# Wd's sums moved to the projection stage, and the last pair of feature tiles multiplied by eight products

## The chip, the cores and the metric

The kernel runs on one core of a Trainium2 chip. The metric is the device time of one execution in microseconds (us). It was measured three times before the change: 2784.34 us is the median, with 2778.39 and 2784.58 beside it. One more execution was taken with the hardware profiler.

Five engines work side by side: TensorE (PE, matmuls; PEld is its weight load), VectorE (DVE), ScalarE (ACT), GpSimd (POOL) and SyncE (SP, which here only issues DMAs). Each runs its instructions in the order in which they were written, and waits at an instruction until its inputs are there.

## The reference

One layer of a trunk model on 2048 rows of width 1024, in float32:

```python
hn = rmsnorm(h, norm_mix[l])
z = hn @ w_in[l]
u_ssm, q, kv, gate_logits, lru_x, lru_g = jnp.split(z, splits, axis=-1)
...
mix = jnp.concatenate([y_ssm, y_nsa, y_lru], axis=-1)
h = h + mix @ w_out[l]
h = h + swiglu(rmsnorm(h, norm_ffn[l]), w_gate[l], w_up[l], w_down[l])
return rmsnorm(h, norm_final)
```

`y_ssm` comes from a diagonal recurrence (the S5 mixer), `y_nsa` from an attention in three branches, `y_lru` from a gated linear recurrence. `swiglu` is `(silu(h @ w_gate) * (h @ w_up)) @ w_down` with 2816 hidden features.

## The kernel before

**Three phases.** `phase_a` projects (`project`, line 492): `z` is made feature tile by feature tile, in passes over blocks of 512 rows, and the two recurrences and the compression of keys run beside it. `phase_b` is the attention and the output projection. `phase_c` (`mlp`, line 1675) is the last part: norm, gate and up, down, final norm. In the profiled execution they take about 0 to 584, 584 to 1370, and 1370 us to the end.

**Products in three parts.** Every operand of a large product is split into a rounded high part and a low part (float32r), and each product is three matmuls: high by high, high by low, low by high. A split costs ACT one copy and DVE or POOL one subtraction.

**Gate, up and down by seven products.** In `phase_c` a pair of feature tiles is handled as a 2 x 2 block product by Winograd's form of Strassen's scheme: seven products instead of eight, with sums of blocks on both sides. The 22 feature tiles of 128 give 11 pairs (`fp`). The 2048 rows are handled in two halves (`s`). For each half, `pair` (line 1852) makes gate and up for the 11 pairs (the gate/up stage), and `down` (line 1981) multiplies the result by Wd. `give` (line 1817) forms the seven combinations of the activations and stores them in DRAM as `gS`. The sums on the side of Wd are the same for both halves: `down_sums` (line 1836) loads two row blocks of Wd into two `nx` tiles of 512 KB, makes four differences of 128 x 512 (two on DVE, two on POOL, in `differences`, line 1708), and stores them as `wS`. It is called once for each of the 11 pairs during the gate/up stage of the first half, with due times 50 + 33 fp. `ahead` (line 1746) uses the same tiles `nx` and `t3` afterwards, and makes the seven row combinations that the second half multiplies.

**The down part.** `down` runs over groups of pairs, `GROUPS_D = (1, 2, 2, 2, 2, 2)`. In a group, `fetch` (line 1900) loads both operands of each of the seven products and splits them; `block` (line 1918) makes the products of one group for one of four row tiles in one PSUM bank and adds the bank to an accumulator `M[k, t]`: 28 banks a group. The accumulators start from the residual stream (`hS`, loaded in `totals`). In the last group `combine` (line 1955) puts the seven accumulators together to row tiles, takes their squares' sum, and `finish` (line 2005) scales them by the final norm and stores them. In the last group of the second half the order is row tile by row tile with all seven products in each (`7 * t + p`), elsewhere product by product (`4 * p + t`).

**What sets the order.** In `phase_a` and `phase_c` every call is recorded as a task with an engine, an assumed cost and a key (its due time). `Plan.run` simulates the engines with these costs: an engine that is free takes, among the tasks that are ready, the one with the lowest key. The order that comes out is the order in which instructions are written to each engine. Tiles of one name form a ring of `bufs` buffers in the order in which they were asked for; a task that takes a buffer waits until all uses of the buffer's last owner are over. In `phase_a` keys count feature units of 24 matmuls (one unit is about 5.4 us); the projection ends at 64.8. DMAs are issued on SP's queue, except a few on POOL's queue in `phase_b`: the loads of `KB` and of the query tiles, which are the first POOL instructions of that phase.

**Names in `phase_a` that matter.** `wsl` is the low part of a projection weight, split on POOL. `stage` is a ring of two tiles through which projected features go to DRAM (`qS`, `kS`, `vS`). The ring `b4` (two tiles of 128 x 1056) and the ring `sA` (two tiles of 128 x 512) serve the S5 mixer (`s5_prep`, `s5_main`).

## Time and profile before

| | us |
|---|---|
| median of three runs | 2784.34 |
| the three runs | 2784.34, 2784.58, 2778.39 |
| the profiled execution | 2778.5 |
| its span | 2776.7 |

| engine | busy us | share of the span |
|---|---|---|
| PE | 2577.2 | 93% |
| DVE | 2296.8 | 83% |
| POOL | 1376.6 | 50% |
| ACT | 1352.3 | 49% |

An engine is busy while it has an instruction in work. Matmuls overlap in the pipeline, so TensorE's busy time is not its rate: the number of matmuls in a stretch says more. A row of a timeline gives start, duration, engine, line, operation, output and inputs; in brackets stand the idle time before it and what ended it. Nearly all lines are 207, the helper that writes the recorded instructions, so groups are told apart by their tiles.

### The profile page before, as it was taken

To read this page: it belongs to the slowest core of one execution; us is meant where nothing else is said; L and a number is where in the kernel's file an instruction comes from. 1 tells how busy PE (TensorE), PEld (TensorE's weight loads), DVE (VectorE), ACT (ScalarE), POOL (GpSimd) and SP (SyncE) were. 2 spreads that over 40 slices of the span, in tenths; PEclk is the share of its full clock that TensorE was granted. 3 is DMA by queue.
4 is the path that set the end of the run, shared out by engine and by line. 5 is a ranking of instruction groups with operands and counts; after the bars stand their busy time and mean duration, and the time that the engine had idled before them with its cause. 6 is when DMAs were issued, how large, how long until landed. Compare 5 with 4: busy or idle time off the path is not lost. (4 is left out here: it accounts for less than half of the span.)

```text
span 2776.7 us, 43054 instructions
## 1 busy us (share of the span) xinstructions
PE 2577.2 (93%) x14889; PEld 2095.7 (75%) x14889; DVE 2296.8 (83%) x4480; ACT 1352.3 (49%) x2820; POOL 1376.6 (50%) x971
## 2 busy tenths in 40 slices
PE   6988889989999999998969989999998999999996
PEld 5756568777887788877758777887886888888785
DVE  8797776259898999999899999878889887877877
ACT  5662433147877777876633323344345333334433
POOL 2445441124544343443266766665466555556446
PEclk9999999979999999999989999999999999999998
DMA  5455556662212121121436665346654233326652
GB/s 170 121 157 161 148 137 199 204 171 61 70 41 64 36 64 41 41 52 41 143 105 227 242 228 198 113 145 239 214 180 148 107 107 113 104 90 235 218 200 82
DMA packets 231706, 376.11 MB, mean 135 GB/s; under 512 B 67040, under 2 KB 114912, under 8 KB 231488
## 3 DMA queue, kind: packets, MB, share of 16 engines
q1 hardware_dynamic: 185456, 339.27, 37.6%
q0 software_dynamic: 43872, 26.22, 4.7%
q10 hardware_dynamic: 2160, 7.87, 0.7%
q8 instruction: 118, 1.93, 0.3%
q14 instruction: 100, 0.82, 0.1%
HBM read 259.84 MB, written 113.44 MB: 134 GB/s over the span
## 5 line engine op out<-in xcount | busy, mean ns | idle before, releaser
L207 PE MATMUL B<-h,al 128*128 128x512 f32 x1232 | 486.7, 395 | 16.7 <-POOL al L207 11.2
L207 PE MATMUL B<-h,ah 128*128 128x512 f32 x1232 | 485.8, 395 | 16.7 <-ACT ah L207 7.1
L207 PE MATMUL B<-l,ah 128*128 128x512 f32 x1232 | 485.0, 394 | 4.5 <-DVE l L207 4.5
L207 PE MATMUL B<-l,h 128*128 128x512 f32 x1848 | 431.6, 394 | 11.7 <-POOL l L207 5.3
L207 PEld LDWEIGHTS B<-l,h 128*128 128x128 f32 x1848 | 348.0, 190 | 88.7 <-POOL l L207 8.2
L207 PEld LDWEIGHTS B<-h,al 128*128 128x128 f32 x1232 | 233.7, 190 | 72.4 <-POOL al L207 15.3
L207 PEld LDWEIGHTS B<-h,ah 128*128 128x128 f32 x1232 | 234.2, 190 | 67.0 <-ACT ah L207 8.2
L207 POOL TENSOR_TENSOR l<-raw,l 128x1024 fp32r<-128x1024 f32 (+1 forms) x84 | 195.8, 2342 | 170.2 <-ACT l L207 144.8
L207 PEld LDWEIGHTS B<-l,ah 128*128 128x128 f32 x1232 | 234.1, 190 | 54.7 <-DVE l L207 6.2
L393 DVE SCALAR_TENSOR_TENSOR ptl<-B,pth 128x512 f16<-128x512 f32 (+3 forms) x408 | 246.1, 624 | 22.4 <-ACT pth L384 21.1
L384 ACT ACTIVATE pth<-B 128x512 f16<-128x512 f32 (+3 forms) x408 | 214.4, 548 | 55.9 <-PE B L1509 31.6
L399 PE MATMUL B<-wo,mix 128*128 128x512 f32 x768 | 227.0, 412 | 4.7 <-DMA mix<-mixS 3.9
L207 ACT ACTIVATE ah<-S 128x512 fp32r<-128x512 f32 x176 | 110.4, 628 | 236.2 <-PE B L207 183.6
L207 POOL TENSOR_TENSOR U<-U,s 128x512 f32<-128x512 f32 x96 | 151.8, 1581 | 102.4 <-DVE U L207 57.3
L207 POOL TENSOR_TENSOR al<-S,ah 128x512 fp32r<-128x512 f32 x92 | 149.0, 1620 | 94.8 <-ACT ah L207 94.8
L384 ACT ACTIVATE Ps<-Ps,mn 128x1024 f32<-128x1024 f32 (+7 forms) x192 | 172.7, 902 | 41.3 <-DVE mn L1412 40.1
L399 PE MATMUL B<-KB,Q 128*128 128x384 f32 (+3 forms) x448 | 185.1, 413 | 6.4 <-DVE im L396 2.1
L207 PE MATMUL B<-hnl,wsh 128*128 128x512 f32 x448 | 183.3, 409 | 1.8 <-DVE hnl L207 1.8
L207 PE MATMUL B<-hnh,wsh 128*128 128x512 f32 x448 | 182.6, 408 | 0.5 <-ACT stage L207 0.3
L1509 PE MATMUL B<-ident,Ps 128*128 128x128 f32 x1088 | 181.1, 277 | 1.2 <-ACT Ps L384 0.8
L207 PE MATMUL B<-hnh,wsl 128*128 128x512 f32 x448 | 179.2, 400 | 0.0
L399 PE MATMUL B<-VV,ptl 128*128 128x64 f16 x1448 | 148.2, 195 | 27.8 <-DVE ptl L393 26.8
(371 smaller groups left out, 6282.1 us busy)
## 6 DMA issues: line engine op xcount, KB each, us to landing
raw<-in_wgu SPq DMA_DIRECT2D x88, 512.0 KB, 3.7
raw<-gS SPq DMA_DIRECT2D x70, 512.0 KB, 3.9
gS<-U SPq DMA_DIRECT2D x88, 256.0 KB, 2.1
raw<-wS SPq DMA_DIRECT2D x40, 512.0 KB, 4.0
gS<-s SPq DMA_DIRECT2D x66, 256.0 KB, 2.1
raw<-in_wd SPq DMA_DIRECT2D x66, 256.0 KB, 3.8
wraw<-in_wzf SPq DMA_DIRECT2D x28, 512.0 KB, 4.4
nx<-in_x SPq DMA_DIRECT2D x24, 512.0 KB, 4.5
```

Of the source, the lines that this page charges most:

```text
L207: f(*[real(x) for x in a], **{n: real(x) for n, x in k.items()})
L384: return self.S.activation(o, i, f, **k)
L393: return (eng or self.V).scalar_tensor_tensor(o, a, s, b, op0=op0, op1=op1, **k)
L399: return self.PE.matmul(o, l, r, start=start, stop=stop)
L1509: self.PE.transpose(pt.v[:, j - a], P.v[:, c:c + 128], self.ident)
```

## The change

The differences of Wd are made in `project`, after all other calls, for the first ten pairs: `self.at(WD_A[0] + WD_A[1] * fp, 0, self.down_sums, fp)`, with keys 60.0 to 60.9. Their loads and stores are issued on POOL's queue; the two loaded blocks stand in `b4` tiles, the fourth tile in `sA`. `wS` is kept for `phase_c`.

The eleventh pair (`TAIL = 10`) needs no sums of Wd: its four activation blocks are stored as they are (`eS`), and `ends` multiplies them by Wd's own rows, in eight products for two row tiles and two column halves at a time. This comes after the last group of seven-product pairs, whose `GROUPS_D` is now `(1, 2, 2, 2, 1, 2)`. The accumulators of the seven products are combined in that last group, ahead of the eleventh pair's products, and each of these is then added to a finished row tile. Two of the combinations move from POOL to DVE. Both halves now run all groups product by product. The row tiles are finished in groups of four, and the last four one by one; the first column half of every row tile but the last is multiplied by the final gain on DVE.

```diff
--- before.py
+++ after.py
@@ -42,12 +42,14 @@
 BANKS_C = {"P": 6, "tr": 2}
 STEP_C = 12 * 0.227
 LEAD_W, LEAD_R, LEAD_G, LEAD_D = 12.0, 40.0, 24.0, 14.0
-GROUPS_D = (1, 2, 2, 2, 2, 2)
+GROUPS_D = (1, 2, 2, 2, 1, 2)
+TAIL = 10
+WD_A = (60.0, 0.1)
 REST_C = 13.0
 GAIN_A = -6.5
 STEP_A = 0.01
 FIRST = ((0, 1), (1, 2), (2, 3), (3, 4))
-LAST = (11, 15)
+LAST = (15,)
 ACC_TAGS = {1: (("ah", 6), ("al", 6)) * 2, 6: (("ah", 6), ("al", 6)) * 2, 5: (("ah", 6), ("al", 6)) * 2, 2: (("S", 4),) * 4,
             7: (("s1", 2), ("s5", 2)) * 2, 3: (("th", 2), ("U2", 2)) * 2, 4: (("U3", 2),) * 2 + (("gain2", 1),) * 2}
 PC_TAGS = (("gain2", D, 1),) + tuple((f"{x}{n}", 2048, 1) for n in (6, 5) for x in "hl") \
@@ -362,6 +364,7 @@
         self.hS = [d(f"hS{i}", [128, D]) for i in range(16)]
         self.gS = [{k: [d(f"gS{s}_{k}_{g}", [128, n, 512]) for g, n in enumerate(GROUPS_D)] for k in range(1, 8)} for s in range(2)]
         self.wS = {k: [d(f"wS{k}_{g}", [128, n, 512]) for g, n in enumerate(GROUPS_D)] for k in (4, 5, 6, 7)}
+        self.eS = [d(f"eS{s}", [2, 128, 2, 512]) for s in range(2)]
         self.tS = [{n: d(f"t{n}{j}", [128, 512]) for n in ("B11", "B21", "B22", "T1", "T2", "T3", "T4")} for j in range(4)]
         self.rS = d("rS", [128, 8, 512])
         self.s5S = d("s5S", [8, 128, 1056])
@@ -450,7 +453,7 @@
 
     def phase_a(self):
         tc = self.tc
-        kept = ("gates", "vmax", "KC", "vcT", "ssq", "uS", "yS", "kcS", "kS", "qS", "vS", "mixS", "rS", "s5S", "s5T")
+        kept = ("gates", "vmax", "KC", "vcT", "ssq", "uS", "yS", "kcS", "kS", "qS", "vS", "mixS", "rS", "s5S", "s5T", "wS")
         with ExitStack() as ctx:
             pool = ctx.enter_context(tc.tile_pool(name="pa", bufs=1))
             psum = ctx.enter_context(tc.tile_pool(name="pa_ps", bufs=1, space=PSUM))
@@ -554,6 +557,33 @@
                     self.at(x - LEAD[2], 0, weights, u[0])
                 self.feat_unit(seq[u[0]], q, hq[v], ws[u[0]])
                 x += 1
+        for fp in range(TAIL):
+            self.at(WD_A[0] + WD_A[1] * fp, 0, self.down_sums, fp)
+
+    def differences(self, a0, b0, a1, b1, t3, names=("T2", "T4")):
+
+        self.tt(t3, b1, a1, OP.subtract)
+        if "T2" in names:
+            self.tt(a1, a1, a0, OP.subtract, eng=self.G)
+            self.tt(a0, a0, t3, OP.add)
+            if "T4" in names:
+                self.tt(b0, b0, a0, OP.subtract, eng=self.G)
+        else:
+            self.tt(b0, b0, a0, OP.subtract, eng=self.G)
+            self.tt(b0, b0, t3, OP.subtract)
+
+    def down_sums(self, fp):
+
+        gi, j = at_group(fp)
+        x = []
+        for i in range(2):
+            x.append(self.pool.tile([128, 1056], F32, name="b4", bufs=2)[:, :D])
+            self.G.dma_start(x[i], self.io["wd"][2 * fp + i])
+        t3 = self.w("sA", bufs=2)
+        a0, a1, b0, b1 = x[0][:, :512], x[0][:, 512:], x[1][:, :512], x[1][:, 512:]
+        self.differences(a0, b0, a1, b1, t3)
+        for k, v in ((7, t3), (5, a1), (6, a0), (4, b0)):
+            self.G.dma_start(self.wS[k][gi][:, j], v)
 
     def bcast(self, t, v):
         self.dma(t, bass.AP(tensor=v.tensor, offset=v.offset, ap=[[0, 128], [1, v.shape[0]]]))
@@ -1670,7 +1700,7 @@
             psum = ctx.enter_context(self.tc.tile_pool(name="pc_ps", bufs=1, space=PSUM, reuse_waits="tile"))
             for name, n, bufs in PC_TAGS:
                 pool.tile([128, n], F32, name=name, bufs=bufs)
-            self.recorded(pool, psum, BANKS_C, ("rstd", "ssq", "hS", "gS", "wS", "tS"), self.mlp, START_C)
+            self.recorded(pool, psum, BANKS_C, ("rstd", "ssq", "hS", "gS", "eS", "wS", "tS"), self.mlp, START_C)
 
     def mlp(self):
 
@@ -1705,16 +1735,7 @@
             self.stt(x, x, r, gain, OP.mult, OP.mult)
             return x
 
-        def differences(a0, b0, a1, b1, t3, names):
...
+        differences = self.differences
 
         def rows_a(j):
 
@@ -1811,14 +1832,14 @@
             self.act(th, g, AF.Tanh, scale=0.5)
             self.stt(g, th, 1.0, g, OP.add, OP.mult)
 
-        def at_group(fp):
-            return (0, 0) if fp == 0 else ((fp + 1) // 2, (fp + 1) % 2)
-
         def give(s, fp, r, c, g, u, G, U):
 
+            self.stt(g, g, 0.5, u, OP.mult, OP.mult)
+            if fp == TAIL:
+                self.dma(self.eS[s][c][:, r], g)
+                return
             gi, j = at_group(fp)
             keep = lambda k, x: self.dma(self.gS[s][k][gi][:, j], x)
-            self.stt(g, g, 0.5, u, OP.mult, OP.mult)
             G[r, c], U[r, c] = g, u
             if (r, c) != (0, 1):
                 keep({(0, 0): 1, (1, 0): 2, (1, 1): 4}[r, c], g)
@@ -1832,19 +1853,6 @@
             if (r, c) == (1, 0):
                 self.tt(u, g, U[1, 1], OP.subtract, eng=self.G)
                 keep(3, u)
-
-        def down_sums(fp):
-
-            gi, j = at_group(fp)
-            x = []
-            for i in range(2):
-                x.append(pool.tile([128, D], F32, name="nx", bufs=3))
-                self.dma(x[i], io["wd"][2 * fp + i])
-            t3 = pool.tile([128, 512], F32, name="t3", bufs=1)
-            a0, a1, b0, b1 = x[0][:, :512], x[0][:, 512:], x[1][:, :512], x[1][:, 512:]
-            differences(a0, b0, a1, b1, t3, ("T2", "T4"))
-            for k, v in ((7, t3), (5, a1), (6, a0), (4, b0)):
-                self.dma(self.wS[k][gi][:, j], v)
 
         PROD = {1: ("A11", "B11"), 2: ("A12", "B21"), 3: ("S4", "B22"), 4: ("A22", "T4"), 5: ("S1", "T1"), 6: ("S2", "T2"),
                 7: ("S3", "T3")}
@@ -1899,11 +1907,14 @@
 
         def fetch(s, k, gi, pos, x):
 
-            n, first, r = GROUPS_D[gi], sum(GROUPS_D[:gi]), []
+            n, first, r = 2 if k is None else GROUPS_D[gi], sum(GROUPS_D[:gi]), []
             for tag in "hl":
                 v = pool.tile([128, 2, D], F32R, name=f"{tag}{FREED[s][pos]}", bufs=1)[:, :, :512 * n]
                 raw = pool.tile([128, KT, 128], F32, name="raw", bufs=4).rearrange("p a b -> p (a b)")[:, :512 * n]
-                if tag == "h" or k in self.wS:
+                if k is None:
+                    src = self.eS[s][gi].rearrange("p a b -> p (a b)") if tag == "h" else io["wd"][2 * TAIL + gi]
+                    self.at(x - LEAD_G, 0, self.dma, raw, src)
+                elif tag == "h" or k in self.wS:
                     src = (self.gS[s] if tag == "h" else self.wS)[k][gi]
                     self.at(x - LEAD_G, 0, self.dma, raw, src.rearrange("p a b -> p (a b)"))
                 else:
@@ -1959,53 +1970,69 @@
             if k == 6:
                 tt(2, 1, G)
                 tt(6, 1)
-                tt(3, 6, G)
+                tt(3, 6)
             elif k == 5:
-                tt(3, 5, G)
+                tt(3, 5)
             elif k == 7:
                 tt(7, 6)
                 tt(4, 7, G)
                 tt(7, 5)
-            i = 8 * s + t
-            for i, dh, o, after in ((i, 0, 2, 2), (i, 1, 3, 3), (i + 4, 0, 4, 4), (i + 4, 1, 7, 7)):
-                if k == after:
-                    a, d = M[o, t], slice(512 * dh, 512 * dh + 512)
-                    acc[i, dh] = a
-                    junk = pool.tile([128, 512], BF, name="junk", bufs=1)
-                    self.at(x + .3, 0, lambda: self.act(junk, a, AF.Square, accum_out=ms[:, dh, col(i):col(i) + 1]))
-                    if i in LAST:
-                        if i not in last:
-                            last[i] = pool.tile([128, D], F32, name="nx", bufs=3)
-                        self.at(x + .3, 0, self.tt, last[i][:, d], a, gfin[dh], OP.mult, self.G if dh else None)
+        def ends(s, i, dh, hw, x):
+
+            c, t = i // 4, i % 4
+            i += 8 * s
+            a, d = M[{(0, 0): 2, (0, 1): 3, (1, 0): 4, (1, 1): 7}[c, dh], t], slice(512 * dh, 512 * dh + 512)
+            ps = psum.tile([128, 512], F32, name="P")
+
+            def products():
+                for r in range(2):
+                    g, w = hw[c][0][:, :, 512 * r + 128 * t:512 * r + 128 * t + 128], hw[r][1][:, :, d]
+                    self.mm(ps, g[:, 0], w[:, 0], r == 0, False)
+                    self.mm(ps, g[:, 0], w[:, 1], False, False)
+                    self.mm(ps, g[:, 1], w[:, 0], False, r == 1)
+
+            self.at(x, 0, products)
+            e = x + 1.362
+            self.at(e, 0, self.tt, a, a, ps, OP.add)
+            acc[i, dh] = a
+            junk = pool.tile([128, 512], BF, name="junk", bufs=1)
+            self.at(e + .3, 0, lambda: self.act(junk, a, AF.Square, accum_out=ms[:, dh, i:i + 1]))
+            if i in LAST:
+                if i not in last:
+                    last[i] = pool.tile([128, D], F32, name="nx", bufs=3)
+                self.at(e + .3, 0, self.tt, last[i][:, d], a, gfin[dh], OP.mult, self.G if dh else None)
 
         def down(s, x):
+
 
             seq = (1, 6, 5, 2, 7, 3, 4)
             totals(s, x)
             for gi, n in enumerate(GROUPS_D):
-                end = gi == len(GROUPS_D) - 1
                 u = .681 * n
-                at = lambda p, t: x + u * (7 * t + p if end and s else 4 * p + t)
-                hw = {k: fetch(s, k, gi, p, at(p, 0)) for p, k in enumerate(seq)}
-                for t, p in ((t, p) for t in range(4) for p in range(7)) if end and s else ((t, p) for p in range(7) for t in range(4)):
-                    k, y = seq[p], at(p, t)
+                hw = {k: fetch(s, k, gi, p, x + 4 * u * p) for p, k in enumerate(seq)}
+                for t, p in ((t, p) for p in range(7) for t in range(4)):
+                    k, y = seq[p], x + u * (4 * p + t)
                     block(s, k, gi, t, hw[k], y)
-                    if end:
+                    if gi == len(GROUPS_D) - 1:
                         combine(s, t, k, y + u)
-                        if s and k == 4:
-                            self.at(y + u + 1, 0, finish, 8 + t, 12 + t)
-                        elif not s and t == 3 and k in (3, 4):
-                            self.at(y + u + 1, 0.01, finish, *range(4 * (k == 4), 4 * (k == 4) + 4))
                 x += 28 * u
+            hw = [fetch(s, None, r, r, x) for r in range(2)]
+            for i in range(8):
+                for dh in range(2):
+                    ends(s, i, dh, hw, x)
+                    x += 1.362
+                if s and i > 3:
+                    self.at(x + 1, 0, finish, 8 * s + i)
+                elif i == 3 or i == 7:
+                    self.at(x + 1, .01, finish, *range(8 * s + i - 3, 8 * s + i + 1))
             return x
 
         M = {}
-        col = lambda i: i if i < 8 else 8 + 2 * (i % 4) + (i - 8) // 4
 
         def finish(*tiles):
 
             n = len(tiles)
-            c = col(tiles[0])
+            c = tiles[0]
             m = ms[:, 0, c:c + n]
             self.tt(m, m, ms[:, 1, c:c + n], OP.add)
             ys = self.rsqrt(pool, m, n, 1.0 / D, bufs=2, root=tiles[0] > 7)
@@ -2020,7 +2047,7 @@
                             self.ts(a, a, y)
                     else:
                         a = acc[i, dh]
-                        if i > 7 and dh == 0:
+                        if dh == 0:
                             self.stt(a, a, y, gfin[dh], OP.mult, OP.mult)
                         else:
                             self.act(a, a, scale=y)
@@ -2051,8 +2078,6 @@
                     plan.floor = 40.0
                     self.at(x + 60, 0.01, self.row_scales, 1, 2)
                     plan.floor = REST_C
-                if s == 0:
-                    self.at(50 + 33 * fp, 0, down_sums, fp)
                 x += 14 * STEP_C
             if s == 0:
                 for j in range(4):
@@ -2062,6 +2087,15 @@
                 for lead, names in ((26, ("B11", "B21")), (14, ("T2", "T1")), (6, ("T3", "B22")), (2, ("T4",))):
                     for j in range(4):
                         self.at(x - lead + 2 * j, 0, rows_of, j, names)
+
+
+def at_group(fp):
+
+    gi = 0
+    while fp >= GROUPS_D[gi]:
+        fp -= GROUPS_D[gi]
+        gi += 1
+    return gi, fp
 
 
 def bucket(dist):
```

## Rows read from the trace of the kernel before

**Rows 1.** The page's part 1: busy time, share of the span and instructions of each engine
```profile
PE 2577.2 (93%) x14889; PEld 2095.7 (75%) x14889; DVE 2296.8 (83%) x4480; ACT 1352.3 (49%) x2820; POOL 1376.6 (50%) x971
```

**Rows 2.** Busy time by stretch (PE, PEld, DVE, ACT, POOL, clock, DMA share, GB/s), gate/up stages
```profile
1455.00:1550.00 95.00, 95.00 (x418) 78.43 (x417) 89.83 (x98) 31.74 (x55) 66.63 (x43) 0.99 0.68 232
...
1550.00:1700.00 150.00, 135.64 (x569) 107.20 (x568) 138.29 (x139) 39.88 (x72) 106.47 (x66) 0.98 0.69 234
...
1700.00:1850.00 150.00, 150.00 (x663) 124.20 (x662) 128.57 (x143) 52.94 (x91) 90.52 (x59) 1.00 0.36 120
...
2130.00:2500.00 370.00, 370.00 (x1634) 306.35 (x1633) 297.85 (x336) 128.38 (x218) 209.69 (x139) 1.00 0.31 109
```

**Rows 3.** Wd's sums in the first gate/up stage: issues by tile (ns, first to last), DMAs
```profile
L207 SPq DMA_DIRECT2D wS<-t x11: 319/327/327, 1459.3 to 1610.2; - x11
...
nx<-in_wd SPq DMA_DIRECT2D x22, 512.0 KB, 4.2
...
wS<-nx SPq DMA_DIRECT2D x33, 256.0 KB, 2.5
```

**Rows 4.** Groups of 1460 to 1700 us that write nx and t: busy, mean ns, idle before
```profile
L207 DVE TENSOR_TENSOR nx<-nx,t 128x512 f32<-128x512 f32 x15 | 15.6, 1041 | 5.5 <-POOL nx L207 5.5
...
L207 DVE SCALAR_TENSOR_TENSOR nx<-nx,rstd,gain 128x1024 f32<-128x1024 f32 x8 | 14.8, 1846 | 4.6 <-DMA nx<-hS 4.6
...
L207 DVE TENSOR_TENSOR t<-nx 128x512 f32<-128x512 f32 x14 | 11.5, 823 | 0.2
...
L207 POOL TENSOR_TENSOR nx<-nx 128x512 f32<-128x512 f32 x30 | 46.4, 1546 | 37.0 <-DVE nx L207 24.9 <-DVE t L207 10.7 <-PE B L207 1.4
```

**Rows 5.** Late projection: busy time by stretch; TensorE's longest wait there; one row of ACT
```profile
366.00:440.00 74.00, 63.93 (x319) 52.98 (x317) 59.57 (x67) 29.05 (x44) 33.40 (x19) 0.93 0.64 167
...
366.00:584.00 218.00, 199.03 (x1085) 167.39 (x1083) 105.72 (x157) 58.09 (x115) 50.47 (x32) 0.96 0.63 179
...
PE B L207 <- DVE l L207: 15.0, 2, 9.3
...
553.11 0.60 ACT L207 ACTIVATE stage<-B 128x512 fp32r<-128x512 f32 x1 [10.70 <-DMA qS<-stage]
```

**Rows 6.** Last matmuls of the S5 mixer; KB's loads on POOL's queue, first use, landing
```profile
L207 PE MATMUL B<-sA,w_glu x12: 590/592/592, 359.8 to 365.2; 128*128 128x512 f32 x12
...
539.37 3.07 POOL L1089 DMA_DIRECT2D KB<-kS  x4
...
L399 PE MATMUL B<-KB,Q x24: 415/454/582, 589.5 to 619.3; 128*128 128x128 f32 x16, 128*128 128x256 f32 x8
...
KB<-kS POOLq DMA_DIRECT2D x2, 1536.0 KB, 14.3
```

**Rows 7.** One group of the second gate/up stage: DVE adding a PSUM bank
```profile
L207 DVE TENSOR_TENSOR U<-B,U 128x512 f32<-128x512 f32 x38 | 25.8, 679 | 1.2 <-POOL U L207 1.2
```

**Rows 8.** From the first half to the second, in order of time
```profile
2111.23 3.43 DVE L207 TENSOR_TENSOR S<-raw 128x512 f32<-128x512 f32 x2
...
2112.02 0.74 PE L207 MATMUL B<-h,ah 128*128 128x512 f32 x1 [2.45 <-ACT ah L207]
...
2112.55 0.63 PE L207 MATMUL B<-l,ah 128*128 128x512 f32 x1
...
2123.42 0.79 PE L207 MATMUL B<-h,ah 128*128 128x512 f32 x1 [4.62 <-ACT ah L207]
...
2125.38 1.73 POOL L207 TENSOR_TENSOR gain<-gain,gf 128x512 f32<-128x512 f32 x1
```

**Rows 9.** The end: one stretch, then rows in order of time
```profile
2700.00:2725.00 25.00, 22.06 (x88) 17.62 (x87) 19.36 (x21) 9.27 (x12) 17.65 (x10) 0.89 0.36 125
...
2720.29 34.49 PE L207 MATMUL B<-l,h 128*128 128x512 f32 x138 [2.94 <-ACT l L207]
...
2766.61 0.68 DVE L207 TENSOR_TENSOR gain<-gain,B 128x512 f32<-128x512 f32 x1
...
2771.46 1.80 SPq L207 DMA_DIRECT2D out<-nx  x4
```

9 lines of the change are left out of this document (removed).

## The prediction

> **What bounds the kernel now.** I read the page's busy shares first, then busy time by stretch, then TensorE's waits and the rows in order of time where a stretch falls short. TensorE is busy for 93% of the span and VectorE (DVE) for 83% [rows 1], so a saving counts only where TensorE runs below its rate. In the second gate/up stage it never does: 1634 matmuls in 370 us are 0.2264 us each, with DVE busy for 80% [rows 2]. I use 0.2264 us as the price of a matmul of 512 columns. The first gate/up stage holds that rate from 1700 us on, where DVE is 86% busy. It falls short from 1550 to 1700: 569 matmuls would need 128.8 us and took 150, a loss of 21.2 us, with DVE 92% busy [rows 2]. Wd's sums lie in that stage: their stores are issued from 1459.3 to 1610.2, one sum every 15.1 us [rows 3]. The four row sets that `ahead` makes follow them. Three other places cost time: the passage from the first half to the second, where TensorE waits 2.45 and 4.62 us for parts of weights [rows 8]; the start of the last group, where 88 matmuls fill only 19.9 of 25 us; and the end, where TensorE is done at 2720.29 + 34.49 = 2754.8 but DVE adds the last bank at 2766.61 [rows 9].
>
> **The change, part by part.** The sum is made against the profiled execution, 2778.5 us (span 2776.7).
>
> *More products.* Before, a half multiplies 7 x 4 x 11 x 3 = 924 matmuls in its down part. After, it is 7 x 4 x 10 x 3 = 840 for ten pairs, and 8 row tiles x 2 column halves x 2 x 3 = 96 for the last pair: 12 more in each half, 24 x 0.2264 = **+5.4 us**, nothing beside it.
>
> *Sums taken out of the first gate/up stage.* Eleven sums leave, each with two operations on DVE, two on POOL, two loads and four stores. From 1460 to 1700 DVE spent 15.6 + 11.5 us on 29 such operations, of which 22 are the sums': 20.6 us. POOL spent 46.4 us on 30, of which 22 are theirs: 34 us [rows 4]. From 1455 to 1700 DVE was busy for 228.1 of 245 us [rows 2]; without 20.6 it is 85%, below the 86% at which TensorE kept its full rate after 1700. So most of the 21.2 us should come back. What is late next is `ahead`: its tiles stand behind the sums' in the ring `nx`, so it moves forward into the stage's start with eight scalings of 1.85 us [rows 4]. I leave it 3 us and take **-18** (bounds -10 and -21: that the crowding keeps half, or nothing).
>
> These DVE operations took 0.82 and 1.04 us on average where one that reads PSUM takes 0.68 [rows 4, 7]. The Trainium skill (SBUF — State Buffer, "Who interferes with whom") says that a DVE instruction with two SBUF inputs and a POOL instruction that reads SBUF block each other for the whole instruction. The longer means agree. By that rule POOL's 34 us would give DVE more than its own 20.6, and the term would lie at its -21 end.
>
> *The ten sums in the late projection.* They add 20 operations on DVE, 20 on POOL and 60 DMAs on POOL's queue. A sum's result tile comes from the ring `sA`, whose users before it are the S5 mixer's last matmuls, at 365 us [rows 6]; so the chain of ten starts at about 366. The two `b4` tiles make it serial: the loads of one sum wait for the stores of the last. A cycle is at least one load's issue and landing (0.77 + 4.2), four operations (0.82 + 1.55 + 1.04 + 1.55), one store's issue and landing (0.77 + 2.5): 13.2 us; with the other four issues in line it is 16.3 [rows 3, 4, 6]. (An issue on POOL's queue is 3.07 / 4 = 0.77 us.) The sums before came every 15.1 us. I take 17, so the chain ends at 366 + 170 = 536. Queued behind it on POOL are the low parts of the projection's weights (`wsl`), for which TensorE waits, and `KB`'s loads: these were issued at 539.4, the larger ones land 14.3 us later, and `KB` is first read at 589.5 [rows 6]. They may start as late as 575, or 20.9 us a sum. Queued behind a waiting sum on DVE are the recurrence's steps, for which TensorE already waits 15.0 us [rows 5].
>
> Engines have room: from 366 to 584 us DVE is busy for 105.7 of 218 and POOL for 50.5 [rows 5], and the sums add about 19 and 77. The transfers have less. 21.0 MB at 0.69 / 234 share per GB/s [rows 2] fill all 16 DMA engines for 62 us, or 0.28 of 218: with the 0.63 there [rows 5] that is 0.91, above every stretch of rows 2. The projection's result tiles (`stage`) waited 10.70 us at 553 for `qS` stores, with `KB`'s 4.2 MB issued on the other queue at 539 [rows 5, 6]. The cost lies between 0 (all beside TensorE's work; below nothing is excluded, since no work leaves this stretch) and 30 (all 18.6 us of DVE's operations on the path, and one more such wait). DVE is crowded, 80%, only in the first 74 us [rows 5], where 4.4 of the ten sums fall: 8.2 us. With 2 for the stores I take **+10**.
>
> The Trainium skill (DMA: Bandwidth & Descriptors, "Issuing engines are not separate DMA queues") says that DMAs of all issuing engines run on the same 16 DMA engines and interleave. The wait of 10.70 us agrees. Were POOL's queue a road of its own, the 2 us would fall away and the time would be 2 us less.
>
> *Groups and combinations.* The fifth group now holds one pair instead of two. There 28 bank adds x 0.679 [rows 7] = 19.0 us of DVE stand against 84 x 0.2264 = 19.0 us of TensorE, so any other DVE operation delays it once PSUM is full: **+2** for both halves (0 to 8). Eight combinations a half go from POOL to DVE, and 16 bank adds are new (10.9 us a half); TensorE's work covers them, as DVE has a seventh to a fifth idle there. The last pair's products no longer make three POOL differences of 1.55 us and three stores ahead of the down part's start: **-3** (0 to -5).
>
> *From half to half.* The seven sums are combined before the last 96 matmuls, so half of the row tiles are finished while TensorE still multiplies, and eight of the sixteen multiplications by the final gain (1.73 us each on POOL) become DVE's. What waited was the S sums (3.43 us for two) beside them [rows 8]. Of 7.1 us I take **-6** (-12, if the slow matmuls of 0.63 us behind the wait go too, to +5, if the new bank adds crowd DVE).
>
> *The end.* The last group no longer runs row tile by row tile, so its seven operand pairs aren't wanted at once: 25 - 19.9 = **-5** (-3 to -5). After TensorE's end DVE was 11.8 us behind. In the last eight products (48 x 0.2264 = 10.9 us) it has 8 adds (5.4) and the finish of eight tiles, which I put at 1.3 each, an estimate from one operation of 0.68 to 1.85 and the short ones [rows 4, 7]: 15.8 us, 5 behind. **-6** (0 to -9).
>
> Sum: 5.4 - 18 + 10 + 2 - 3 - 6 - 5 - 6 = -20.6 us. 2778.5 - 20.6 = 2757.9. The median shown, 2784.3, lies 5.8 above the profiled execution, and the three runs' mean 3.9 above: I forecast **2761 us**.
>
> **The rivals.**
> (a) The sums hide wholly: DVE and POOL are idle for half and three quarters of that stretch [rows 5]. Then the +10 is 0: 2751, down to 2738 with the passage at its best. Against it: TensorE's waits on DVE there.
> (b) A new wait takes the place of the old. Either `ahead`, pushed forward, keeps the loss of 21.2 us (-18 becomes -3: 2776), or the projection's transfers and `wsl` splits stand behind the sums for 25 to 30 us (2776 to 2781). For it: 92% DVE while `ahead` ran [rows 2]; a DMA share of 0.91. Against it: DVE at 85% in total.
> (c) Slower: POOL's queue is overrun. If fuller DMA engines stretch a cycle beyond 20.9 us, `KB`'s loads start after 575 and attention starts late, one for one. At 25 us a sum the chain ends at 616, `KB` lands at 630, 41 us after its first use: 2761 + 41 = 2802. For it: the cycle has four DMA latencies on it and the share nears 1. Against it: 15.1 us at a share of 0.68 before.
> (d) The change doesn't do what it says: the plan puts the sums behind the last `wsl`, so that they start at 539 and end at 709: 134 us later than `KB` is wanted, 2895. The ring is free at 365 and POOL idle, which speaks against it.
>
> **How the numbers follow.** A measurement of this kernel can tell about 0.3% (8.4 us) from no change: the runs before spread by 0.2%. Forecast (2751 to 2776): 0.48. (a), 2736 to 2751: 0.20. (b), within 0.3%, 2776 to 2793: 0.19. (c) 0.11 and (d) 0.02, slower. So faster 0.68, same 0.19, slower 0.13. The range 2738 to 2790 leaves out (c), (d), the top of (b) and a little of (a).
>
> **What would show it.** In the profile after: stores to `wS` on POOL's queue from about 370 to 540, every 16 to 19 us; `KB`'s loads issued before 575 and first read within 10 us of 589.5; in the first gate/up stage 4.4 matmuls a us from 1550 us on; no gap before the last group; DVE's last bank add about 5 us after TensorE's end. The forecast is wrong if attention starts over 15 us later, if `ahead` brings back a DVE above 90% with TensorE short, or if the one-pair group shows DVE as TensorE's releaser for more than a few us.

## The result and the profile after

The changed kernel takes 2822.2 us (four runs, 2821.9 to 2827.3), the kernel before 2784.1 beside it: ratio 1.0146, 95% interval 1.0128 to 1.0164. The forecast was 2761 in a range of 2738 to 2790: the measured time lies outside it, on the other side of no change. The profiled executions are 2778.5 us before and 2822.3 after, spans 2776.7 and 2820.5, so 43.8 us have to be found.

Their places follow from the first and last TensorE products of each stage in the two traces (us; "gap" lies between the last down product of the first half and the second half's first; tail is from TensorE's last product to the end of the span; ends of matmuls are modelled, so -0.2 is no gap):

| | before | after | difference |
|---|---|---|---|
| first gate/up product | 1392.9 | 1428.4 | +35.5 |
| first gate/up stage | 474.7 | 459.6 | -15.1 |
| first down part | 226.1 | 241.5 | +15.4 |
| gap and second gate/up stage | 438.9 | 441.5 | +2.6 |
| second down part | 222.1 | 232.2 | +10.1 |
| tail | 21.9 | 17.4 | -4.5 |

The sum is +44.0. The start of attention alone accounts for the first line: `KB` is first read at 625.2 us where it was 589.5 [rows 6], +35.7.

First the sums in the late projection. In the trace after, the issues of wS's stores by tile (min/median/max ns, first and last start), and the stretches of [rows 5] (PE, PEld, DVE, ACT, POOL, clock, DMA share, GB/s):

```profile
L209 POOL DMA_DIRECT2D wS<-b x30: 540/543/586, 379.4 to 598.5; - x30
L209 POOL DMA_DIRECT2D wS<-sA x10: 579/582/744, 377.3 to 595.1; - x10
...
366.00:440.00 74.00, 62.37 (x280) 48.07 (x279) 53.75 (x65) 25.86 (x37) 46.33 (x37) 0.91 0.70 208
366.00:584.00 218.00, 187.85 (x927) 148.59 (x926) 120.96 (x166) 56.37 (x102) 102.00 (x97) 0.93 0.73 232
```

The stores of t3 run from 377.3 to 595.1: nine cycles of 24.2 us, where 17 was taken and 20.9 was the most that `KB` could bear. TensorE did 927 matmuls up to 584 us rather than 1085. What a cycle waits for stands on POOL's and DVE's timelines after; this is the ninth sum, which of the nine behind the first waits longest for DVE:

```profile
559.27 0.54 POOL L209 DMA_DIRECT2D b<-in_wd  x1 [0.43 <-DMA wS<-b]
576.24 1.28 POOL L209 TENSOR_TENSOR b<-b 128x512 f32<-128x512 f32 x1 [16.43 <-DVE sA L209]
...
597.46 1.63 POOL L209 DMA_DIRECT2D wS<-b  x3
599.08 2.87 POOL L1119 DMA_DIRECT2D KB<-kS  x4
601.90 1.30 POOL L1294 DMA_DIRECT2D Q<-qS  x2
603.12 1.58 POOL L1297 DMA_DIRECT2D QB<-qS  x2
```

```profile
566.85 0.69 DVE L209 SCALAR_TENSOR_TENSOR stage<-B,stage 128x512 fp32r<-128x512 f32 x1 [13.95 <-ACT stage L209]
574.87 0.69 DVE L209 SCALAR_TENSOR_TENSOR stage<-B,stage 128x512 fp32r<-128x512 f32 x1 [7.33 <-ACT stage L209]
575.47 0.68 DVE L209 TENSOR_TENSOR sA<-b,b 128x512 f32<-128x512 f32 x1
```

Wd's second tile is asked for at 559.3 and landed at 563.7; the sum's first operation runs on DVE only at 575.5, though DVE is idle most of the time: in its queue the operation stands behind two `stage` operations of the projection, which wait for ACT (13.95 and 7.33 us), as ACT waits for TensorE's products. POOL waits 16.43 us for it, and everything behind it on POOL waits too: KB's loads go out at 599.1 (539.4 before [rows 6]) and those of Q behind them.

The other cycles wait less for DVE. On average over the nine, 5.9 us pass from a sum's last store to the issue of the next sum's second load, 5.6 to its landing, 4.1 till DVE begins, 6.6 for the four operations with the waits between them, and 2.0 to the last store's issue: 24.2. TensorE after:

```profile
604.04 0.29 PE L209 MATMUL B<-wth,hnl 128*128 128x280 f32 x1
...
620.44 1.01 PE L1320 MATMUL B<-KC,Q 128*128 128x8 f32 x4 [11.04 <-DMA Q<-qS]
624.29 1.02 PE L1322 MATMUL B<-KC,QB 128*128 128x8 f32 x4 [2.83 <-DMA QB<-qS]
625.17 0.45 PE L402 MATMUL B<-KB,Q 128*128 128x128 f32 x1
```

The projection's last matmul starts at 604.0; before, at 582.5. So 21.5 us of the 35.7 are a slower projection, and the other 14.2 a wait for Q (11.04) and QB (2.83), which stood behind the ten sums and KB on POOL's queue.

The slower projection has two parts. Up to its last matmul, before and after, and then two short stretches after (columns as above):

```profile
0.00:583.00 583.00, 511.82 (x2406) 389.45 (x2406) 391.11 (x732) 224.67 (x407) 204.62 (x190) 0.96 0.56 160
0.00:604.00 604.00, 519.16 (x2405) 391.32 (x2406) 405.53 (x751) 224.35 (x407) 264.57 (x270) 0.94 0.59 182
...
500.00:550.00 50.00, 39.92 (x200) 31.79 (x199) 20.44 (x27) 4.46 (x10) 19.48 (x19) 1.00 0.78 251
550.40:560.60 10.20, 10.20 (x18) 4.92 (x16) 1.12 (x2) 2.25 (x4) 5.71 (x8) 0.50 0.74 249
```

The matmuls are the same. TensorE is idle for 84.8 us rather than 71.2, 13.6 more, and busy for 7.3 us more, with a mean granted clock of 0.94 rather than 0.96: about a third of the 21.5 goes with the clock. Weighted by the granted clock, the busy time is the same, 494.5 and 494.8 us. At 550.4 it fell to 0.50, the lower of its two levels (1.2 rather than 2.4 GHz), for 10.2 us, after 50 us of which TensorE had been busy for 39.9. None of TensorE's waits from 366 us on is for `wsl`.

Executions differ here: in six traces with the projection of the kernel before, order and all, its last matmul starts at 578.5 to 589.0 us, and in six with all ten sums as in the changed kernel at 604.0 to 606.7. So the ten sums' delay is clear, and a difference of a few us between two traces is not.

The gate/up stage answers [rows 2]:

```profile
1455.00:1550.00 95.00, 85.31 (x368) 68.89 (x368) 90.03 (x104) 28.65 (x50) 60.76 (x38) 0.93 0.57 194
1550.00:1700.00 150.00, 146.19 (x638) 120.40 (x637) 130.75 (x144) 49.79 (x85) 94.32 (x61) 0.99 0.42 139
1700.00:1850.00 150.00, 150.00 (x664) 124.20 (x663) 117.76 (x136) 52.10 (x88) 82.72 (x55) 1.00 0.31 103
```

From 1550 us on it has 638 matmuls in 150 us rather than 569 (the stage's slow start now lies in the first line, 36 us later than before). In the first down part TensorE waits after for DVE (longest sums of waits, times, longest one; the first row is the gap):

```profile
PE B L209 <- ACT h L209: 7.2, 1, 7.2
PE B L209 <- DVE ah L209: 6.5, 3, 2.6
PE B L209 <- DVE al L209: 4.6, 3, 2.8
PE B L209 <- DVE U L209: 3.5, 3, 1.6
PE B L209 <- DVE s L209: 3.4, 2, 2.5
```

In the second half's last group, one stretch of DVE's timeline, and POOL's beside it:

```profile
2747.14 0.68 DVE L209 TENSOR_TENSOR al<-al,B 128x512 f32<-128x512 f32 x1
2747.74 1.19 DVE L209 TENSOR_TENSOR th<-th,ah 128x512 f32<-128x512 f32 x1
2748.85 2.89 DVE L209 TENSOR_TENSOR al<-al 128x512 f32<-128x512 f32 x1
2751.66 0.67 DVE L209 TENSOR_TENSOR ah<-ah,B 128x512 f32<-128x512 f32 x1
2752.26 2.27 DVE L209 TENSOR_TENSOR U<-U,al 128x512 f32<-128x512 f32 x1
...
2748.34 5.65 POOL L209 TENSOR_TENSOR l<-raw,l 128x1024 fp32r<-128x1024 f32 x2
```

DVE has no idle time, and bank adds (`<-al,B`) alternate with the combinations that came from POOL (`th<-th,ah`, `U<-U,al`), of up to 2.27 us, and with one of 2.89 (`al<-al`) that was on DVE before too. TensorE waits four times there; the end is then shorter than before [rows 9], the last bank add 3.5 us behind TensorE's last product (2764.30 + 38.83 = 2803.1):

```profile
2764.30 38.83 PE L209 MATMUL B<-l,h 128*128 128x512 f32 x162 [2.83 <-DVE al L209]
```

```profile
2806.62 0.67 DVE L209 TENSOR_TENSOR s<-s,B 128x512 f32<-128x512 f32 x1
```

### The profile page after: what moved, and what is told of

It reads as the page before. It is cut to its first block, busy times and chain, and to the rows that moved or that the text cites. A ratio compares the mean times of both kernels' runs of the same rounds, so it can differ in the third digit from the quotient of the medians.

```text
span 2820.5 us, 43111 instructions
## 1 busy us (share of the span) xinstructions
PE 2589.2 (92%) x14913; PEld 2103.5 (75%) x14913; DVE 2297.2 (81%) x4541; ACT 1347.8 (48%) x2821; POOL 1354.7 (48%) x1003
## 4 chain that ended last, share of the span: by engine, by line
PE 57%; DVE 23%; DMA 8%; issue 5%; POOL 4%; ACT 3%; SPq 1%; POOLq 0%; DVEq 0%; ACTq 0%
PE B L209 41%; PE B L402 11%; DVE l L209 4%; PE B L1539 4%; DVE ptl L396 3%; DVE Ps L1442 2%; POOL l L209 2%; DMA raw<-wS 1%; DVE S L209 1%; DVE nx L209 1%; DVE al L209 1%; DMA raw<-gS 1%; DVE acc L396 1%; DVE h L209 1%; DMA l<-kcS 1%
## 5 line engine op out<-in xcount | busy, mean ns | idle before, releaser
L209 PE MATMUL B<-h,ah 128*128 128x512 f32 x1232 | 484.8, 394 | 19.4 <-DVE l L209 11.5
L209 PE MATMUL B<-l,h 128*128 128x512 f32 x1872 | 438.4, 394 | 35.0 <-DVE ah L209 9.4
L209 POOL TENSOR_TENSOR U<-U,s 128x512 f32<-128x512 f32 x92 | 139.8, 1519 | 127.9 <-DVE s L209 57.9
L209 DVE TENSOR_TENSOR h<-raw,h 128x1024 fp32r<-128x1024 f32 (+1 forms) x88 | 133.1, 1512 | 72.5 <-ACT h L209 72.5
L387 ACT ACTIVATE Ps<-Ps,mn 128x1024 f32<-128x1024 f32 (+7 forms) x192 | 172.6, 901 | 40.6 <-DVE mn L1442 39.3
```

The lines of the kernel that those rows point to most:

```text
L209: f(*[real(x) for x in a], **{n: real(x) for n, x in k.items()})
L387: return self.S.activation(o, i, f, **k)
```

## The experiments

The theory after reading: the move of the sums costs 36 us ahead of attention and gives back 15 behind it, and the changed down parts cost the rest. All times are compared with the kernel before, run beside them (medians 2784 to 2788 us); stage lengths come from the traces as in the table above.

| run | KB first read | first gate/up product | gate/up 1 | down 1 | gap | gate/up 2 | down 2 | tail | time | ratio to before (95%) |
|---|---|---|---|---|---|---|---|---|---|---|
| before | 589.5 | 1392.9 | 474.7 | 226.1 | -0.2 | 439.1 | 222.1 | 21.9 | 2784.1 | 1 |
| after | 625.2 | 1428.4 | 459.6 | 241.5 | 9.9 | 431.6 | 232.2 | 17.4 | 2822.2 | 1.0146 (1.0128, 1.0164) |
| sums_in_c | 585.5 | 1389.6 | 471.5 | 241.5 | 9.9 | 430.5 | 232.8 | 17.7 | 2799.9 | 1.0049 (1.0034, 1.0064) |
| sums_only | 627.3 | 1433.0 | 465.4 | 227.4 | -0.2 | 439.7 | 223.9 | 22.2 | 2812.2 | 1.0092 (1.0077, 1.0107) |
| sums_5_5 | 603.5 | 1408.5 | 469.4 | 240.1 | 9.9 | 430.6 | 230.6 | 17.6 | 2809.1 | 1.0090 (1.0073, 1.0107) |
| sums_off_pool | 604.3 | 1410.3 | 460.1 | 239.6 | 9.9 | 432.4 | 234.6 | 17.6 | 2805.5 | 1.0077 (1.0062, 1.0092) |
| transfers_only | 597.9 | 1402.4 | 459.7 | 241.7 | 9.8 | 431.4 | 232.8 | 17.7 | 2797.3 | one run |
| comb_pool | 625.0 | 1429.3 | 462.6 | 234.9 | 9.9 | 431.5 | 230.2 | 17.5 | 2820.8 | 1.0134 (1.0113, 1.0155) |
| groups_22222 | 627.3 | 1430.8 | 462.3 | 223.4 | 9.9 | 432.4 | 221.6 | 17.3 | 2799.7 | 1.0055 (1.0040, 1.0070) |
| groups_112222 | 627.6 | 1430.4 | 462.7 | 243.8 | 9.9 | 431.7 | 241.2 | 17.5 | 2839.0 | 1.0181 (1.0165, 1.0196) |
| ends_tags | 627.3 | 1432.9 | 460.1 | 243.5 | -0.2 | 431.5 | 236.2 | 17.4 | 2821.5 | 1.0136 (1.0121, 1.0151) |
| before_spread | 591.7 | 1396.8 | 475.0 | 230.5 | -0.2 | 440.2 | 222.3 | 22.0 | 2786.8 | 1.0007 (0.9998, 1.0016) |
| down_mended | 588.5 | 1392.4 | 470.7 | 229.8 | -0.2 | 433.3 | 222.4 | 17.6 | 2769.7 | 0.9953 (0.9936, 0.9969) |
| down_mended_pool | 596.0 | 1398.8 | 471.9 | 229.6 | -0.2 | 433.2 | 214.2 | 17.6 | 2765.7 | 0.9933 (0.9918, 0.9948) |
| down_mended_close | 590.1 | 1393.9 | 471.8 | 223.8 | -0.2 | 433.2 | 216.5 | 17.6 | 2760.1 | 0.9901 (0.9883, 0.9918) |

### Two halves of the change apart

**sums_in_c.** The ten sums go back to the first gate/up stage, on SP's queue and in tiles of the ring `nx`; the rest of the change stays.

```diff
-        for fp in range(TAIL):
+        for fp in range(0):
             self.at(WD_A[0] + WD_A[1] * fp, 0, self.down_sums, fp)
...
+                if s == 0 and 0 <= fp < TAIL:
+                    self.at(50 + 33 * fp, 0, sums_c, fp)
                 x += 14 * STEP_C
```

> The changed kernel with its ten sums put back where they were, between the row tiles of the first gate/up stage; the last pair's eight products, the groups 1,2,2,2,1,2 and the combinations stay as changed. Theory A (the loss has two parts: the sums' move costs 36 us at the start of attention and gives back 16 in the first gate/up stage, and the changed down part costs the other 24): attention's first KB matmul at 589 to 591 us, time about 2822 - 36 + 16 = 2802. Rival B (the down part is worth the 13 us that I forecast for it, and all of the loss comes from the sums' move, part of it by transfers pushed elsewhere): 2778 - 13 = 2766.

Measured 2799.9: theory A. KB is read at 585.5, the gate/up stage is back at 471.5, and the down parts stay at 241.5 and 232.8. The forecast's gain in the down part (rival B) does not exist.

**sums_only.** The kernel before, and only the ten sums moved.

```diff
+        for fp in range(TAIL):
+            self.at(WD_A[0] + WD_A[1] * fp, 0, self.down_sums, fp)
...
-                if s == 0:
+                if s == 0 and fp >= TAIL:
                     self.at(50 + 33 * fp, 0, down_sums, fp)
```

> The kernel before with only the move: ten of its eleven sums run in the late projection exactly as in the changed kernel (POOL's queue, two b4 tiles, same keys), the eleventh stays in the first gate/up stage; groups, combinations and the end as before. Theory A: attention 36 us late, 16 us won in the gate/up stage: 2778 + 20 = 2798. Rival B: all of the loss is here and the down part hides 13 of it: 2835.

Measured 2812.2, 14 above theory A and 23 below B. KB is read 37.8 us late, gate/up starts 40.1 late, wins 9.3 rather than 15 (one sum is still in it), and the down parts keep before's 227 and 224. The two halves measured apart, 26.4 and 14.2 us by the medians, make 40.6 of the 38.1 that they cost together: the loss is theirs, with hardly any interplay.

### The late projection

**sums_5_5.** Five sums in the late projection, five in the first gate/up stage.

```diff
-        for fp in range(TAIL):
+        for fp in range(5):
             self.at(WD_A[0] + WD_A[1] * fp, 0, self.down_sums, fp)
...
+                if s == 0 and 5 <= fp < TAIL:
+                    self.at(50 + 33 * fp, 0, sums_c, fp)
```

> The changed kernel with five sums in the late projection and five in the first gate/up stage. Theory A (the late start of attention is 21.5 us of a late projection and 14.2 us of Q's loads that stand behind the chain of sums on POOL's queue): five cycles of 24 us end at about 497, KB is issued at 540 as before and Q is not waited for, the projection loses about half, so attention's first KB matmul at 590 to 601; half of the 16 us of gate/up is lost again: 2822 - 26 + 8 = 2804. Rival C (each sum costs the same 3.6 us wherever it stands, by its transfers alone): 2822 - 18 + 8 = 2812.

```profile
544.55 2.85 POOL L1119 DMA_DIRECT2D KB<-kS  x4
```

Measured 2809.1, between the two. The half of A on the queue holds: the chain ends at 492 us, KB is issued at 544.6 and nothing is waited for but the projection. But this is 14.2 us late with five sums where it is 21.5 with ten: more than half, which A did not expect. Whether the first sums, in the crowded start of the stretch, cost more than the later ones is not shown: one trace's excess over half is 3.4 us, less than the spread of the projection's end.

**sums_off_pool.** The same ten sums, all four operations on DVE and the transfers on SP's queue.

```diff
-            self.G.dma_start(x[i], self.io["wd"][2 * fp + i])
+            self.dma(x[i], self.io["wd"][2 * fp + i])
...
-        self.differences(a0, b0, a1, b1, t3)
+        for o, p, q, op in ((t3, b1, a1, OP.subtract), (a1, a1, a0, OP.subtract), (a0, a0, t3, OP.add), (b0, b0, a0, OP.subtract)):
+            self.tt(o, p, q, op)
...
-            self.G.dma_start(self.wS[k][gi][:, j], v)
+            self.dma(self.wS[k][gi][:, j], v)
```

> The changed kernel with the same ten sums in the same stretch, but nothing of them on POOL: all four operations on DVE, loads and stores on SP's queue. The same bytes move. Theory A: KB and Q are issued at about 540 and not waited for, the projection stays about 20 us late because the sums stand in DVE's and the transfers' way: attention's first KB matmul at about 611, 2822 - 14 = 2808. Rival D (POOL's queue is the whole cause, the wsl splits behind the sums included): first KB matmul near 590, 2822 - 36 = 2786. Rival E (the stores of the projection's result tiles now stand behind the sums' loads on SP's queue): later than 625, above 2822.

```profile
532.08 3.07 POOL L1120 DMA_DIRECT2D KB<-kS  x4
```

Measured 2805.5: theory A, with `KB` read at 604.3 where it said 611. With the same bytes and the same number of operations, KB goes out at 532 and the wait for Q is gone; the projection's last matmul starts at 597.2, still 14.7 us late. So taking the sums off POOL, operations and queue together, is worth 20.9 of the 35.7 us: the wait of 14.2 and 6.8 of the projection's 21.5, less 0.1.

**transfers_only.** As sums_off_pool, without the four operations (Wd's own columns are stored in place of the sums).

```diff
-        t3 = self.w("sA", bufs=2)
...
-        self.differences(a0, b0, a1, b1, t3)
-        for k, v in ((7, t3), (5, a1), (6, a0), (4, b0)):
-            self.G.dma_start(self.wS[k][gi][:, j], v)
+        for k, v in ((7, b1), (5, a1), (6, a0), (4, b0)):
+            self.dma(self.wS[k][gi][:, j], v)
```

> The changed kernel with the sums' loads and stores on SP's queue and their four operations left out, so that what is stored to wS is Wd itself and the down part multiplies other numbers: the same bytes move in the late projection, and neither DVE nor POOL does anything for them. With the operations on DVE (the run sums_off_pool) the projection's last matmul ended at 597.2 us, 14.7 after the kernel before. Theory A (the transfers delay the projection): it ends at 593 to 600. Rival B (the sums' 40 operations stand in the way of the projection's own on DVE): 582 to 586.

```profile
L209 SPq DMA_DIRECT2D wS<-b x40: 319/450/1925, 274.6 to 411.5; - x40
...
591.07 0.29 PE L209 MATMUL B<-wth,hnl 128*128 128x280 f32 x1
```

Between the two: 591.1 us, but the run doesn't decide. Without the fourth tile the chain no longer waits for the ring `sA`: its stores run from 274.6 to 411.5, not from 377 on, so the same bytes move in another, earlier stretch. And it is one execution, 2.1 us above the latest of those without any sum (589.0). How the 14.7 us that are left in sums_off_pool divide between the transfers, the operations on DVE and the clock stays open.

### The first gate/up stage

**before_spread.** The kernel before; its sums and `ahead` get earliest times, so that they spread over the stage.

```diff
+                    plan.floor = 45.0 + 33 * fp
                     self.at(50 + 33 * fp, 0, down_sums, fp)
+                if s == 0 and fp % 2 and fp < 9:
+                    plan.floor = 62.0 + 33 * fp
+                    self.at(60 + 33 * fp, 0, ahead, fp // 2)
```

> The kernel before with the order of one thing changed: the eleven sums of Wd and the four steps of ahead (rows of the second half) get earliest times of their own, one sum in every 33 units of the first gate/up stage and one step of ahead after every second sum; before, all of them ran between 1455 and 1700 us, where DVE is busy for 93% and TensorE loses 21 us, and from 1700 to 1850 DVE has a seventh idle. No work is added or removed. Theory A (the loss is the crowding, so it can be had without moving the sums to another stage): the stage takes 455 to 462 us rather than 474.7, 2784 - 15 = 2769. Rival B (each of these operations costs TensorE the same wherever it stands, by DVE's and POOL's operations holding each other up): 472 to 477 us, 2784.

```profile
1455.00:1550.00 95.00, 92.46 (x397) 75.37 (x398) 90.41 (x97) 29.48 (x51) 56.81 (x36) 0.97 0.50 175
1550.00:1700.00 150.00, 142.92 (x616) 115.66 (x615) 131.32 (x140) 42.15 (x75) 102.95 (x65) 0.99 0.57 195
1700.00:1850.00 150.00, 143.66 (x626) 116.59 (x625) 132.86 (x142) 47.59 (x85) 101.25 (x64) 1.00 0.55 186
```

Rival B: 475.0 us. The edit spreads the sums (stores to wS from 1464 to 1828 us rather than from 1459 to 1623). From 1550 to 1700 TensorE does 616 matmuls rather than 569 [rows 2], and from 1700 to 1850 626 rather than 663: the loss moves with the sums. DVE is busy for 88% there and TensorE still waits. So spreading the load on DVE wins nothing, and DVE at 92%, the reason that the prediction gave for its -18, is not shown to be what costs. Eleven sums left the stage with the change, 1.4 us each (15.1 / 11); from sums_in_c to the changed kernel it is 1.2 (11.9 / 10). What TensorE waits for, before and then spread (1500 us to the stage's end), is `al`, the low parts of one side's operands, which POOL and DVE make:

```profile
PE B L207 <- POOL al L207: 10.2, 6, 3.2
PE B L207 <- DVE al L207: 4.1, 5, 2.2
...
PE B L207 <- DVE al L207: 8.8, 7, 2.7
PE B L207 <- POOL al L207: 4.9, 3, 1.9
```

14.3 us before and 13.7 spread; more than two thirds of the first are POOL's, where each sum has two operations too. Which part of a sum delays them wasn't tried.

### The down part

**comb_pool.** The combinations M3 += M6 and M3 += M5 on POOL again.

```diff
-                tt(3, 6)
+                tt(3, 6, G)
...
-                tt(3, 5)
+                tt(3, 5, G)
```

> The changed kernel with the eight combinations of a half that the change gave to DVE (M3 += M6, M3 += M5) back on POOL. In the changed kernel TensorE waits 9.4 us in the first half's last group and 7.5 us in the second's for bank adds that stand behind these combinations on DVE. Theory A (DVE is the bound there): each down part shortens by 6 to 8 us, 2822 - 14 = 2808. Rival B (POOL's slower combinations delay the same tiles' last adds by as much): within 3 us of 2822.

The time, 2820.8, says B; the down parts of the one trace are 6.6 and 2.0 us shorter, as A in the first half. The first gate/up stage, 3.0 us longer, doesn't answer it: its order is the changed kernel's, and in traces of this order it takes 459.6 to 462.7. The combinations are the smaller part of the down parts' loss.

**groups_22222.** Five groups of two.

```diff
-GROUPS_D = (1, 2, 2, 2, 1, 2)
+GROUPS_D = (2, 2, 2, 2, 2)
```

> The changed kernel with its ten pairs in five groups of two, no group of one pair. A group costs 28 bank adds of 0.68 us on DVE whatever its size, so DVE has 19 us less to do in each half; TensorE's products are the same. Theory A (the down parts of 241.5 and 232.2 us are long because DVE comes late with bank adds): 5 to 9 us less each, 2822 - 14 = 2808. Rival B (the first group, now of two pairs, must load and split twice as much before it starts, and the gap goes there): each down part starts 4 to 6 us late, 2822 - 4 to 2822 + 6.

```profile
PE B L209 <- DVE ah L209: 5.3, 1, 5.3
PE B L209 <- DVE th L209: 1.3, 1, 1.3
PE B L209 <- POOL l L209: 0.5, 1, 0.5
```

Measured 2799.7, 22.5 us under the changed kernel where A said 14: the down parts fall by 18.1 and 10.6 us, to 223.4 and 221.6, and of TensorE's waits in the first one only a few stay. The first group's double load (rival B) costs nothing that is seen. In the first down part DVE's bank adds fall from 111.7 to 94.4 us, while the operands' splits on DVE take 62.6 and 64.3, so these are not what was won.

**groups_112222.** The second group of one pair moved to the front.

```diff
-GROUPS_D = (1, 2, 2, 2, 1, 2)
+GROUPS_D = (1, 1, 2, 2, 2, 2)
```

> The changed kernel with the second group of one pair moved from fifth to second place; ten pairs, six groups and the same number of bank adds. In the changed kernel the first half's down part loses about 10 us in its first three groups and about 9 in the last; with five groups of two both losses were gone (223.4 rather than 241.5 us). Theory A (the fifth place is what costs: DVE comes out of the group of one pair with its adds behind, straight into the combinations): the last group loses 2 us or less and the first half's down part takes 230 to 234 us, the second's 224 to 228. Rival B (28 more bank adds are what costs, wherever they stand): 240 and 231, with the loss now in the first three groups.

Measured 2839.0: rival B, and more in the second half, 243.8 and 241.2 us. Of TensorE's waits in the first down part 7.0 us still lie in the last group, where B had put all of them into the first three. It isn't the fifth place; the number of groups costs, and with it the count of bank adds. A group empties 28 banks whatever its size (12 of the first group's on ACT, the others by adds of 0.68 us on DVE), and the last pair's eight products 16: 6 x 28 + 16 = 184 in the changed kernel, 168 before, 156 with five groups. The first down part takes 241.5, 226.1 and 223.4 us.

**ends_tags.** The last pair's operands of the first half in h3 and h4.

```diff
-            hw = [fetch(s, None, r, r, x) for r in range(2)]
+            hw = [fetch(s, None, r, r if s else 3 + r, x) for r in range(2)]
```

> The changed kernel with one difference in the first half: the operands of the last pair's eight products sit in the tiles h3 and h4 (and l3, l4) rather than h0 and h1. h0 and h1 are the first two operands of the second half's gate/up products. Theory A (the 9.9 us gap from half to half is these two tiles: they come free only after the last product): the gap closes, at most a gap of 2 us stays, 2822 - 8 = 2814. Rival B (the gap is DVE's and ACT's work beside it, the S sums or the finish of eight row tiles, as I had it in the prediction): the gap stays within 2 us of 9.9, 2822.

After, and then in ends_tags, the second half's first product:

```profile
2139.30 1.22 PE L209 MATMUL B<-h,ah 128*128 128x512 f32 x2 [7.24 <-ACT h L209]
```

```profile
2129.80 6.74 PE L209 MATMUL B<-l,h 128*128 128x512 f32 x29
2136.37 0.39 PE L209 MATMUL B<-h,ah 128*128 128x512 f32 x1
```

The gap closes wholly, as A says, so the two tiles were its cause. The time does not follow: 2821.5, the down parts 2.0 and 4.0 us longer and the first gate/up product 4.5 us later than in the changed kernel. The edit comes behind that point in the work; between runs whose projection is the same text, that start lies from 1428.4 to 1432.9, so that part is spread, and a gain of this size is near what one run can show.

### Together

**down_mended.** Sums in the first gate/up stage and spread, five groups of two, h3 and h4.

```diff
-GROUPS_D = (1, 2, 2, 2, 1, 2)
+GROUPS_D = (2, 2, 2, 2, 2)
...
+                if s == 0 and fp < TAIL:
+                    plan.floor = 45.0 + 35 * fp
+                    self.at(50 + 33 * fp, 0, sums_c, fp)
...
+            hw = [fetch(s, None, r, r if s else 3 + r, x) for r in range(2)]
```

> The changed kernel with the sums back in the first gate/up stage but spread as in the run before_spread, ten pairs in five groups of two, and the first half's last operands in h3 and h4. Theory A (parts add up): attention starts as before (first gate/up product at 1390), gate/up 455 to 462 us, down parts of 223 and 222, no gap, second gate/up 431, end 17: 1390 + 459 + 224 + 431 + 222 + 17 = 2743 in the span, 2750 in the time, 1.2% under the kernel before. Rival B (the crowding comes back and the gap's time is given back in the second half, as in ends_tags): 2770.

Measured 2769.7, as rival B in size, 0.47% under before; but there is no gap and the second down part has its 222. What theory A had wrong are 459 us for the gate/up stage (470.7: spreading wins nothing here either) and 224 for the first down part (229.8).

**down_mended_pool.** The same with the edit of comb_pool.

> The run down_mended with the eight combinations of a half back on POOL. Theory A (what they cost on DVE, 6.6 and 2.0 us in the two down parts of comb_pool, is their crowding with the group of one pair): nothing is won where that group is gone, within 3 us of down_mended. Rival B (they cost DVE's time in the last group whatever is ahead of them): 5 to 8 us less than down_mended.

2765.7, 3.9 less, between A and B. The first down part doesn't change and the second is 8.2 us shorter (B there). In the profiled execution a start 6.4 us later takes most of it; the work ahead of that start is the same, and it lies from 1389.6 to 1398.8 in the traces without sums there, so this is spread.

**down_mended_close.** The same without the spreading: `ahead` behind all sums, as before.

> The run down_mended_pool with the sums not spread but in the order of the kernel before, ahead after them. Theory A (the order of the sums in the first gate/up stage doesn't matter, as before_spread showed): the stage within 3 us of 471.9 and the time within 4 us of 2766. Rival B (spread sums reach into the first down part and lengthen it, 229.6 us against 223.4 in groups_22222): 5 to 7 us less, 2760.

2760.1, ratio 0.9901 (0.9883, 0.9918): 1.0% less than the kernel before. Gate/up takes 471.8 (A), the first down part 223.8 (B): spread sums lengthen it, as in before_spread (230.5 where it was 226.1). In this first down part TensorE waits for only:

```profile
PE B L209 <- DVE th L209: 3.4, 1, 3.4
PE B L209 <- POOL l L209: 0.2, 1, 0.2
```

## Why the prediction failed

**Sums out of the gate/up stage, -18.** Measured -15.1, in its bounds, but not for the reason given: with the same work spread out and DVE less crowded nothing came back (before_spread). So as far as the runs show, the size came out by luck.

**Ten sums in the late projection, +10 (0 to 30).** Measured +35.7, above its upper bound. The first store at 377 fits a chain that starts soon after 366, and the outcome named as rival (c) came about: cycles of 24.2 us against its 25, KB late on POOL's queue. It was given 0.11, for the cycle was added up from issues, landings and operations, 16.3 us, as if DVE took each operation at once. The step that failed is there: I named what stands behind a waiting sum on DVE, and not what a sum stands behind. DVE's first operation came 4.1 us after the landing on average, half of the 7.9 us that the cycle was too long, and 11.8 us in the one shown; the landings and the waits between the four operations made the rest. Fuller DMA engines, the reason that (c) gave, can be no more than a part of that: their share from 366 to 584 us rose to 0.73 and not to the estimated 0.91, while KB's loads and the last sum came behind 584. Rival (c) had the price of one cause only, 41 us for KB; measured were 14.2 for Q's loads and 21.5 for the projection itself, of which 6.8 went when the sums left POOL. The bound of 30 allowed for DVE's operations and one more wait of TensorE, and for no clock: some 7 of the 21.5 us went with it. Rival (b)'s `wsl` splits were not what TensorE waited for.

**Group of one pair, +2 (0 to 8); down start, -3; last group, -5.** With 5.4 for more products, the two down parts were to be 0.6 shorter in all; they are 25.5 longer. The mis-sized term is the first: the prediction weighed 28 adds of 0.68 us against the group's 19.0 us of TensorE and saw a tie. Dropping that group won 28.7 us (18.1 + 10.6). The last group's -5 did not come either: in the second half TensorE waits 7.5 us for DVE there. DVE carries the operands' splits besides, and 16 more adds and eight combinations for which "TensorE's work covers them" was written, from a seventh of idle time in other stages. Two groups of the first down part after (busy us, mean ns, idle before):

```profile
L209 DVE TENSOR_TENSOR U<-U,al 128x512 f32<-128x512 f32 x4 | 5.9, 1472 | 0.0
...
L209 DVE TENSOR_TENSOR th<-th,ah 128x512 f32<-128x512 f32 x4 | 3.2, 806 | 0.0
```

The eight took 9.1 us, not 8 x 0.68 = 5.4. In the rows of 2748 us an operation with two SBUF inputs took 2.89 beside POOL's `l<-raw,l`, while the bank adds around it kept 0.67 and 0.68. The Trainium skill (SBUF — State Buffer, "Who interferes with whom") says that a DVE instruction with two SBUF inputs contends with a POOL instruction that reads SBUF, and that one with at most one SBUF input, outside the 2-port perf modes, does not. These rows agree; the prediction drew on that rule for the gate/up stage and not for the operations that the change itself brought to DVE.

**From half to half, -6 (-12 to +5).** Measured +2.6 with the second gate/up stage, which got 7.5 us shorter by itself while a gap of 9.9 opened. The gap's cause, the last pair's operands in the tiles that the next half wants first, was in the diff and not in the prediction; ends_tags shows it.

**The end, -6 (0 to -9).** Measured -4.5, with the last bank add 3.5 us behind TensorE where 5 was said: right.

So the term ahead of attention missed by 25.5 us (35.5 for 10), those of the down parts by 26.1 (25.5 for -0.6), half to half by 8.6, the gate/up stage by 2.9 and the end by 1.5: 64.6 in all, which takes the sum of 2757.9 to 2822.5. One smaller sum of the prediction does not come out: under rival (a), 2751 less 6 for the passage at its best is 2745, not 2738. Nothing above rests on it.
